# A hybrid attention and mLSTM encoder layer: v transposes two steps later, the mLSTM state split one step earlier, attention's v gathered ahead of its scores

## Chip, core and metric

The kernel runs on one core of one Trainium2 chip. The core has TensorE (PE in the profile, with its weight loads shown apart as PEld), VectorE (DVE), ScalarE (ACT), GpSimd (POOL) and SyncE (SP), whose queue issues all of this kernel's DMAs. Matmuls write into PSUM, eight banks of 128 x 512 floats; everything else lives in SBUF or in DRAM. The metric is the time of one execution on the device in microseconds. Three runs of the kernel before gave 2636.76 us in the median (2635.14 to 2638.74).

## What is computed

One layer of an encoder on two sequences, 1024 tokens (prompt) and 256 tokens (sample), model width 2048. Two groups of heads work side by side on one projection of the normalised input.

```python
hn = rmsnorm(x, norm_w)
proj = jnp.einsum('btd,dp->btp', hn, w_in)            # 2048 -> 9232 columns
na_q, na_k, na_v, na_g, ml_qk, ml_v, ml_o, ml_z, ml_gp = jnp.split(proj, cuts, axis=-1)
att = neighbourhood_attention(na_q, na_k, na_v, na_rpb)   # 8 heads of 128, windows of 8 x 16 on a grid 64 wide
att = att * jax.nn.silu(na_g)
qk = jax.nn.silu(centred_depthwise_conv(ml_qk, conv_w, conv_b))
mq, mk = jnp.split(qk, 2, axis=-1)                    # 4 heads of 256
h = bidirectional_mlstm(mq, mk, mv, gates)            # chunks, forward and backward, state C carried over chunks
mem = rmsnorm(h, head_norm_w) * sigmoid(ml_o) * silu(ml_z)
y = rmsnorm(x + concat(att, mem) @ w_out)
```

The mLSTM output of a chunk is the sum of a part inside the chunk, `p @ v`, and a part from the state carried in, `q @ C_prev`; both once forward and once backward. All of it is float32.

## The kernel before

**Precision.** To multiply float32 on TensorE, each operand is split into a high part, rounded to fp32r, and a low part, the remainder; three products (high x high, high x low, low x high) are added up. `split` (L149) makes the two parts: one copy on ACT, one subtraction on DVE. Nearly every operand goes through such a split, so a matmul waits for a DMA, then ACT, then DVE.

**Stages.** The span has three stages.

*Stage 1* (0 to about 1114 us) projects the first 768 tokens, two blocks of 128 columns at a time. `pair_a` (L314) makes one pair with seven sums of products in seven PSUM banks (three tagged `pr`, four of the five tagged `a`), in four rounds r over the contraction. In each round it goes through the seven banks; for each it splits a weight block and issues six products. In the last round `fold` adds the banks up on DVE into the result tiles `Cn` (two tiles of tag `pc`, of five) and scales them (`out_scaled`, L161). What is left to do with a pair is returned as a generator, `finish_a` (L284), and driven inside the next pair: after the banks 5, 4 and 2 of the rounds 0 to 2 `pair_a` calls `next(bg, None)` once (L380), nine steps in all, and what then remains runs behind the last round. For the eight v pairs (n1 = 56, 58, ... 70) `finish_a` has six steps: each transposes 128 tokens of the two result tiles on TensorE into the spare `a` bank (L308), copies them on ACT (L310) and stores them (L311). The pairs run in the order qk, v, rest, rest, eight times.

*Stage 2* (about 1114 to 2222 us) projects the remaining 512 tokens (`proj_v` L578, `proj_pair` L497) and does attention and mLSTM. For each of four head groups the projections come first; then `run` (L1132) takes two streams of units: the mLSTM of one head (sample, then prompt: four state units and four output units) and the attention of two heads (`na_sample`, `na_prompt`). A unit is a generator; in each turn of `run` every stream starts one more unit, and every unit already started makes one step, the newest first. So a `yield` says in which turn, and behind which other unit, an instruction is written.

*Stage 3* (about 2222 us to the end) is the output projection; the edits don't touch it.

**What sets the order.** The program is written once from top to bottom, and every instruction gets a rank in that order; what `run` writes stands under `tc.high_priority()` (L1135) and ranks ahead of all projections. A planner in the framework (`schedule_with_timeline_sim=True`, L1461) then walks through an estimated timeline and puts, on each engine, the highest-ranking instruction that it takes to be ready next. It also hands out the tiles: a tag has a fixed number of tiles, and an instruction whose tile isn't free yet is not placed until an earlier user of one is. The order so made is fixed: on the chip each engine, and SP's queue, runs its list in order and waits at its head.

**Tiles around the change.** In stage 2 mLSTM units share eight tiles of tag `hf` (L600): an output unit takes three for k, v and q, and two for the split states `Cf` (forward) and `Cr` (backward, named Cb in the profile). The state units take from the same eight. Attention's raw loads share two tiles of tag `nraw`: q and k of a head (`setup`, L686), v of a sample head, and the v gather of a block. The split v has two tiles of tag `nv`, the bias table two of tag `nbt`.

**The steps of the units.** An output unit (`out_unit`, L979) has four: load and split k, v, q (mlp_Jk, mlp_Jv, mlp_Jq); scores (mlp_Js) and the weighted in-chunk matrix (mlp_Jd, mlp_Jp); state update (L1031), state split, the products with the state (mlp_Jin) and inside the chunk (mlp_Jacc), and the normalisation (mlp_Jx, mlp_Jr, mlp_Jhs); transposes and the gate (mlp_Jtp, mlp_Jzr). An attention block (`block`, L706) has three: scores and softmax (nap_0s, nap_0st) with the gather of v; transposes of the probabilities (nap_0t, nap_0pt); the product with v (nap_0o).

Of the kernel before, what the change touches and what calls it, by code (L numbers as in the profile page):

```python
# [9 lines left out]
F32R = mybir.dt.float32r  # L10
# [3 lines left out]
P = 128  # L14
# [3 lines left out]
TP = 1024  # L18
# [20 lines left out]
def kernel(  # L39
# [17 lines left out]
    V, S, G, PE, DM = nc.vector, nc.scalar, nc.gpsimd, nc.tensor, nc.sync  # L57
# [8 lines left out]
    def bank(tag, name):  # L66
        return ps.tile([P, 512], F32, tag=tag, name=name, bufs=3 if tag == "pr" else 5)

    pT = [dram.tile([P, TT], F32, tag=f"pT{n}", name=f"pT{n}") for n in range(NCH)]
    vD = [dram.tile([TT, 256], F32, tag=f"vD{u}", name=f"vD{u}") for u in range(NU)]  # L70
# [78 lines left out]
    def split(hi, lo, src, scale=None):  # L149
        if scale is None:  # L150
            S.copy(hi, src)  # L151
            V.tensor_tensor(lo, src, f(hi), op=ALU.subtract)  # L152
        else:
            S.mul(hi, src, scale)
            V.scalar_tensor_tensor(lo, src, scale, f(hi), op0=ALU.mult, op1=ALU.subtract)
# [34 lines left out]
    def pc(name):  # L190
        return wa.tile([P, GA], F32, tag="pc", name=name, bufs=NPC)
# [75 lines left out]
    def conv_taps(dst, src, ct, n, pad):  # L267
        S.activation(
            dst[:, :n], src[:, 2 - pad : 2 - pad + n], AF.Identity,
            bias=cb_sb[:, ct : ct + 1], scale=cw_sb[:, ct, 2:3],  # L270
        )
        for j in (0, 1, 3, 4):
            a = max(pad - j, 0)
            V.scalar_tensor_tensor(  # L274
                dst[:, a:n], src[:, a + j - pad : n + j - pad], cw_sb[:, ct, j : j + 1],
                dst[:, a:n], op0=ALU.mult, op1=ALU.add,
            )
            yield
        S.activation(src[:, :n], dst[:, :n], AF.Tanh, scale=0.5)
        V.scalar_tensor_tensor(  # L280
            dst[:, :n], src[:, :n], 1.0, dst[:, :n], op0=ALU.add, op1=ALU.mult
        )

    def finish_a(n1, Cn):  # L284
        nm = f"A{n1}"
        for j in range(2):
            if n1 >= NCH:
                break
            if QK0 <= n1 < OT0:
                ct = n1 - QK0 + j  # L290
                DM.dma_start(qb[ct], Cn[j][:, GA - 4 :])
                cv = pc(f"{nm}cv{j}")
                yield from conv_taps(cv, Cn[j], ct, GA - 2, 2)
                DM.dma_start(cD[ct][:, : GA - 2], cv[:, : GA - 2])
            else:
                if OT0 <= n1 < ZT0:
                    S.activation(Cn[j], Cn[j], AF.Tanh, scale=0.5)
                elif n1 >= GT0:
                    th = pc(f"{nm}th{j}")
                    S.activation(th, Cn[j], AF.Tanh, scale=0.5)  # L300
                    V.scalar_tensor_tensor(Cn[j], th, 1.0, Cn[j], op0=ALU.add, op1=ALU.mult)
                DM.dma_start(pT[n1 + j][:, 0:GA], Cn[j])
            yield
        if n1 >= NCH:
            for tt in range(GA // P):
                b = bank("a", f"{nm}v{tt}")
                for j in range(2):
                    PE.transpose(b[:, j * P : (j + 1) * P], Cn[j][:, tt * P : (tt + 1) * P], ident)  # L308
                o = wa.tile([P, 256], F32, tag="vo", name=f"{nm}vo{tt}", bufs=2)
                S.copy(o, b[:, :256])  # L310
                DM.dma_start(vD[(n1 - NCH) // 2][tt * P : (tt + 1) * P, :], o)  # L311
                yield
# [287 lines left out]
    def hf(name):  # L600
        return ap.tile([P, 1032], F32R, tag="hf", name=name, bufs=8)
# [7 lines left out]
    def na_tile(tag, shape, name, bufs, dt=F32):  # L609
        return ap.tile(shape, dt, tag=tag, name=name, bufs=bufs)  # L610
# [71 lines left out]
    def na_prompt(h):  # L682
        nm = f"nap{h}"
        hd = {}

        def setup():  # L686
            t = na_tile("nqk", [P, 4, TP], f"{nm}qk", 1, F32R)
            q, k = ([t[:, 2 * i + z] for z in range(2)] for i in range(2))
            for half in range(2):
                cs = slice(half * 512, half * 512 + 512)  # L690
                for w_, t, src in (("q", q, pT[QT0 + h]), ("k", k, pT[KT0 + h])):
                    raw = na_tile("nraw", [P, 512], f"{nm}{w_}r{half}", 2)
                    DM.dma_start(raw, src[:, cs])
                    if w_ == "q":
                        d = [
                            x_[:, cs].rearrange("p (b r c) -> p r b c", b=4, c=16) for x_ in t
                        ]
                        split(*d, raw.rearrange("p (r b c) -> p r b c", b=4, c=16))
                    else:
                        split(t[0][:, cs], t[1][:, cs], raw)  # L700
            o = na_tile("not", [P, TP], f"{nm}o", 1)
            DM.dma_start(o[:, :GA], pT[GT0 + h][:, :GA])
            hd["q"], hd["k"], hd["o"] = q, k, o
            yield

        def block(c4):  # L706
            q, k = hd["q"], hd["k"]
            n2 = f"{nm}_{c4}"
            kc = KC0[c4]
            kv = [x_.rearrange("p (r c) -> p r c", c=64) for x_ in k]  # L710
            st = [
                na_softmax(
                    f"{n2}_{rh}",
                    lambda a_: q[a_][:, rh * 512 + c4 * P : rh * 512 + (c4 + 1) * P],
                    lambda b_: kv[b_][:, 4 * rh : 4 * rh + 12, kc : kc + 32],
                    NAK, h, (BKIND[c4] * 2 + rh) * NAK,
                )
                for rh in range(2)
            ]
            v = na_tile("nv", [P, 2, 512], f"{n2}v", 2, F32R)  # L720
            raw = na_tile("nraw", [P, 512], f"{n2}vr", 2)
            vs = vD[h // 2][:TP, (h % 2) * P : (h % 2 + 1) * P].rearrange("(r c) d -> r c d", c=64)
            for m in range(4):
                DM.dma_start(raw[:, m * P : (m + 1) * P], vs[4 * m : 4 * m + 4, kc : kc + 32, :])
            split(v[:, 0], v[:, 1], raw)
            yield
            pt = na_tile("npt", [P, 2, 768], f"{n2}pt", 1, F32R)
            for rh in range(2):
                na_transpose(
                    f"{n2}_{rh}", st[rh], ((1, 2, 0), (0, 1, 2))[rh],  # L730
                    [
                        pt[:, z].rearrange("p (s r q) -> p s r q", r=2, q=P)[:, :, rh, :]
                        for z in range(2)
                    ],
                )
            yield
            b = bank("a", f"{n2}o")
            parts = ((1, 0, 256, 0), (2, 256, 256, 0), (0, 512, P, 0), (3, 640, P, P))
            for j, (m, src, n, o) in enumerate(parts):
                for i, (a_, b_) in enumerate(((0, 0), (0, 1), (1, 0))):  # L740
                    PE.matmul(  # L741
                        b[:, o : o + n], v[:, a_, m * P : (m + 1) * P], pt[:, b_, src : src + n],
                        start=j == 0 and i == 0, stop=j == 3 and i == 2,
                    )
            ov = hd["o"].rearrange("p (r c) -> p r c", c=64)
            bv = b[:, :256].rearrange("p (r c) -> p r c", c=16)
            cs = slice(c4 * 16, c4 * 16 + 16)
            ng = GA // 64
            V.scalar_tensor_tensor(
                ov[:, :ng, cs], bv[:, :ng], 0.5, ov[:, :ng, cs], op0=ALU.mult, op1=ALU.mult  # L750
            )
            S.copy(ov[:, ng:, cs], bv[:, ng:])
            if c4 == 3:
                DM.dma_start(mixT[h][:, :TP], hd["o"])
            yield

        yield setup()
        for c4 in range(4):
            yield block(c4)
# [133 lines left out]
    def ml_units(sq, h, gates):  # L893
# [31 lines left out]
        def c_split(name, src):  # L925
            t = hf(name).rearrange("p (h t c) -> p h t c", h=2, c=VW)
            split(t[:, 0], t[:, 1], src)
            return t
# [50 lines left out]
        def out_unit(J):  # L979
            n2 = f"{nm}_{J}"  # L980
# [18 lines left out]
            for st in range(2):  # L999
# [7 lines left out]
                for d in range(2):  # L1007
# [17 lines left out]
                    split(ph[:, 0], ph[:, 1], dd)  # L1025
                    for e in range(lo_ // P, hi_ // P):
                        pp[d, e, st] = ph[:, :, e * P - lo_ : (e + 1) * P - lo_]
            yield
            if J > 0:
                if J > 1:  # L1030
                    V.scalar_tensor_tensor(  # L1031
# [3 lines left out]
                Cf = c_split(f"{n2}Cf", kvf[J - 1])  # L1035
            if J in Cb:
                Cr = c_split(f"{n2}Cb", Cb[J])
            acc = {}
            for d in range(2):
                hc = d * 4 + h  # L1040
# [26 lines left out]
            r = ap.tile([P, 8], F32, tag="smr", name=f"{n2}r", bufs=4)  # L1067
            for e in range(2):
                for d in range(2):
                    hc = d * 4 + h  # L1070
                    c = e * 2 + d
# [48 lines left out]
        for J in range(nc_):  # L1120
            yield out_unit(J)
# [344 lines left out]
```

## Time and profile before

| | us |
|---|---|
| median of three runs | 2636.76 |
| profiled execution, its own time | 2639.76 |
| span of the profiled execution | 2637.7 |
| TensorE busy, of the span | 2582.4 |
| weight loads busy | 2364.1 |
| VectorE busy | 1923.2 |
| ScalarE busy | 1309.2 |
| GpSimd busy | 709.1 |

The profile is of one execution. Its rows give an instruction group with its line in the code, what it writes and reads, how often, its busy time and mean duration, and, behind a bar, how long the engine stood idle just before it and what ended that wait. A timeline row begins with the start in us from the span's start and the duration; a bracket gives the idle time before it and its releaser. SPq is SP's queue while it issues DMAs. The end of a matmul is modelled, so TensorE's busy share says less than the starts of its instructions and the waits of the weight path.

### The profile page before, as it was taken

To read this page: it belongs to the slowest core of one execution; us is meant where nothing else is said; L and a number is where in the kernel's file an instruction comes from. 1 tells how busy PE (TensorE), PEld (TensorE's weight loads), DVE (VectorE), ACT (ScalarE), POOL (GpSimd) and SP (SyncE) were. 2 spreads that over 40 slices of the span, in tenths; PEclk is the share of its full clock that TensorE was granted. 3 is DMA by queue.
4 is the path that set the end of the run, shared out by engine and by line. 5 is a ranking of instruction groups with operands and counts; after the bars stand their busy time and mean duration, and the time that the engine had idled before them with its cause. 6 is when DMAs were issued, how large, how long until landed. Compare 5 with 4: busy or idle time off the path is not lost.

```text
span 2637.7 us, 42477 instructions
## 1 busy us (share of the span) xinstructions
PE 2582.4 (98%) x14470; PEld 2364.1 (90%) x14470; DVE 1923.2 (73%) x3744; ACT 1309.2 (50%) x2988; POOL 709.1 (27%) x951
## 2 busy tenths in 40 slices
PE   8999999999999999999999999999999999999998
PEld 8999999999999999988998998989888888787777
DVE  7858778787878778774586587677566644989796
ACT  7534444444444444543565566566566423344435
POOL 0434444444444444300011011010000000436232
PEclk9999999999999999999999999999999999999999
DMA  6423333233333232444655646655554567445327
GB/s 209 150 77 118 107 124 112 95 99 101 95 96 109 77 114 91 163 122 147 193 158 172 198 146 190 201 154 177 186 183 150 178 227 278 158 124 189 103 78 254
DMA packets 215648, 389.10 MB, mean 148 GB/s; under 512 B 26976, under 2 KB 116232, under 8 KB 215432
## 3 DMA queue, kind: packets, MB, share of 16 engines
q1 hardware_dynamic: 215432, 386.40, 46.0%
q8 instruction: 114, 1.87, 0.3%
q14 instruction: 102, 0.84, 0.1%
HBM read 314.94 MB, written 71.38 MB: 146 GB/s over the span
## 4 chain that ended last, share of the span: by engine, by line
PE 45%; DVE 8%; DMA 4%; ACT 2%; issue 1%; SPq 1%; POOL 0%; ACTq 0%; POOLq 0%; DVEq 0%
PE pc L497 21%; PE po L1300 10%; PE pv L578 4%; DVE mo L152 2%; DVE wo L152 1%; PE A54b L188 1%; DMA wr<-in_w_in_dram 1%; DVE ms L1214 1%; PE A52b L188 1%; DVE y L1250 1%; PE nap_0s L615 1%; PE nap_1s L615 1%; DMA nap_0vr<-vD 0%; DVE mb L1237 0%; PE nap_2o L741 0%
## 5 line engine op out<-in xcount | busy, mean ns | idle before, releaser
L1300 PE MATMUL po<-wo,mo 128*128 128x512 f32 x1620 | 381.0, 395 | 12.5 <-DVE wo L152 9.9
L1300 PEld LDWEIGHTS po<-wo,mo 128*128 128x128 f32 x1620 | 303.8, 188 | 88.9 <-DVE wo L152 14.9
L152 DVE TENSOR_TENSOR ws<-wr,ws 128x512 fp32r<-128x512 f32 x224 | 153.3, 695 | 119.3 <-ACT ws L151 118.0
L151 ACT CAST ws<-wr 128x512 fp32r<-128x512 f32 x224 | 136.6, 619 | 179.1 <-PE pc L497 116.8
L151 ACT CAST mo<-mb 128x640 fp32r<-128x640 f32 x72 | 51.8, 725 | 108.1 <-PE po L1300 92.4
L152 DVE TENSOR_TENSOR mo<-mb,mo 128x640 fp32r<-128x640 f32 x72 | 72.9, 1023 | 38.8 <-ACT mo L151 38.8
L1250 DVE TENSOR_TENSOR y<-y,po 128x512 f32<-128x512 f32 x90 | 57.6, 678 | 12.8 <-PE po L1300 12.8
L151 ACT CAST mo<-ms 128x640 fp32r<-128x640 f32 x40 | 29.0, 725 | 70.8 <-PE po L1300 32.5
L102 POOL TENSOR_SCALAR mls_0r<-mls_0r 128x2 f32<-128x2 f32 x4 | 1.2, 289 | 234.0 <-ACT mls_0jk L1087 234.0
L152 DVE TENSOR_TENSOR mo<-ms,mo 128x640 fp32r<-128x640 f32 x40 | 48.5, 1214 | 13.2 <-ACT mo L151 13.2
L1265 POOL TENSOR_TENSOR y<-y,fnb 128x512 f32<-128x512 f32 x30 | 48.1, 1621 | 36.3 <-ACT jk L1263 35.8
L152 DVE TENSOR_TENSOR wsv<-wr_v,wsv 128x512 fp32r<-128x512 f32 x64 | 44.0, 693 | 17.5 <-ACT wsv L151 16.8
L151 ACT CAST wsv<-wr_v 128x512 fp32r<-128x512 f32 x64 | 38.9, 617 | 30.8 <-PE pc L497 19.2
L165 DVE TENSOR_TENSOR pco<-pc,rstdb 128x512 f32<-128x512 f32 x48 | 32.8, 686 | 27.8 <-PE pc L497 26.1
L1227 POOL TENSOR_TENSOR wb_0a<-wb_0a,wb_0b 128x512 f32<-128x512 f32 x2 | 2.6, 1302 | 179.5 <-DMA wb_0b<-in_w_o_dram 179.5
L274 DVE SCALAR_TENSOR_TENSOR pcv<-pco,cw_sb,pcv 128x516 f32<-128x516 f32 x64 | 46.7, 749 | 0.0
L1214 DVE TENSOR_TENSOR ms<-mb,mb 128x640 f32<-128x640 f32 x40 | 45.1, 1127 | 0.0
L1263 ACT ACTIVATE jk<-y 128x512 f32<-128x512 f32 x40 | 25.2, 631 | 39.7 <-DVE y L1250 38.2
L497 PE MATMUL pc<-x_0h,ws 128*128 128x512 f32 x112 | 36.5, 406 | 0.9 <-DVE pco L165 0.9
L497 PE MATMUL pc<-x_2h,ws 128*128 128x512 f32 x112 | 35.3, 399 | 0.0
L188 PE MATMUL fb<-xb,fw 128*128 128x384 f32 x96 | 24.7, 374 | 10.8 <-ACT xb L158 10.8
L188 PE MATMUL fb<-xg,fw 128*128 128x384 f32 x192 | 35.1, 336 | 0.1
(1701 smaller groups left out, 8268.9 us busy)
## 6 DMA issues: line engine op xcount, KB each, us to landing
wr<-in_w_in_dram SPq DMA_DIRECT2D x112, 512.0 KB
wr_v<-in_w_in_dram SPq DMA_DIRECT2D x32, 512.0 KB
xq<-in_xtok_dram SPq DMA_DIRECT2D x20, 512.0 KB
mb<-mx SPq DMA_DIRECT2D x32, 320.0 KB
y<-in_xtok_dram SPq DMA_DIRECT2D x40, 256.0 KB
wr_wp<-in_w_o_dram SPq DMA_DIRECT2D x16, 512.0 KB
xr<-in_xT_dram SPq DMA_DIRECT2D x16, 384.0 KB
nap_0bt<-in_rpb_tab_dram SPq DMA_DIRECT2D x32, 192.0 KB
```

What stands on the lines that cost most here:

```text
L151: S.copy(hi, src)
L152: V.tensor_tensor(lo, src, f(hi), op=ALU.subtract)
L165: V.tensor_tensor(o, src, rb, op=ALU.mult)
L188: PE.matmul(o, w(a_), x(b_), start=first and m == 0, stop=last and m == 2)
L274: V.scalar_tensor_tensor(dst[:, a:n], src[:, a + j - pad : n + j - pad], cw_sb[:, ct, j : j + 1], dst[:, a:n], op0=ALU.mult, op1=ALU.add,)
L497: PE.matmul(pb[j], t[j][:, wi, c : c + P], xs[xi], start=first and m == 0, stop=last and m == 2,)
L578: PE.matmul(outs[tt], xs[:, tt * P : (tt + 1) * P], t[:, wi, q * w : (q + 1) * w], start=first and m == 0 and (gates or tt % 2 == 0), stop ...
L615: PE.matmul(b[:, :nkeys], qs(a_), ks(b_), start=i == 0, stop=i == 2)
L1214: V.tensor_tensor(t, x, y_, op=op)
L1250: V.tensor_tensor(Y[p, q, tt], Y[p, q, tt], bk, op=op)
L1265: G.tensor_tensor(Y[p, q, tt], Y[p, q, tt], fnb[c], op=ALU.mult)
L1300: PE.matmul(bk[tt], m[xi][:, tt * P : (tt + 1) * P], w[wi], start=first and kk == 0 and j == 0, stop=last and j == 2, skip_group_check=True,)
```

## The change

There are three edits. The number of instructions is the same; only their place in the program's order changes.

```diff
@@ finish_a
         if n1 >= NCH:
+            yield
+            yield
             for tt in range(GA // P):
                 b = bank("a", f"{nm}v{tt}")
@@ block (attention of a prompt head)
             kv = [x_.rearrange("p (r c) -> p r c", c=64) for x_ in k]
+            v = na_tile("nv", [P, 2, 512], f"{n2}v", 2, F32R)
+            raw = na_tile("nraw", [P, 512], f"{n2}vr", 2)
+            vs = vD[h // 2][:TP, (h % 2) * P : (h % 2 + 1) * P].rearrange("(r c) d -> r c d", c=64)
+            for m in range(4):
+                DM.dma_start(raw[:, m * P : (m + 1) * P], vs[4 * m : 4 * m + 4, kc : kc + 32, :])
             st = [
                 na_softmax(
...
                 for rh in range(2)
             ]
-            v = na_tile("nv", [P, 2, 512], f"{n2}v", 2, F32R)
-            raw = na_tile("nraw", [P, 512], f"{n2}vr", 2)
-            vs = vD[h // 2][:TP, (h % 2) * P : (h % 2 + 1) * P].rearrange("(r c) d -> r c d", c=64)
-            for m in range(4):
-                DM.dma_start(raw[:, m * P : (m + 1) * P], vs[4 * m : 4 * m + 4, kc : kc + 32, :])
+            yield
             split(v[:, 0], v[:, 1], raw)
-            yield
             pt = na_tile("npt", [P, 2, 768], f"{n2}pt", 1, F32R)
@@ out_unit (mLSTM)
                         pp[d, e, st] = ph[:, :, e * P - lo_ : (e + 1) * P - lo_]
-            yield
             if J > 0:
                 if J > 1:
                     V.scalar_tensor_tensor(
...
                 Cf = c_split(f"{n2}Cf", kvf[J - 1])
             if J in Cb:
                 Cr = c_split(f"{n2}Cb", Cb[J])
+            yield
             acc = {}
```

Edit 1: the generator of a v pair makes two empty steps first, so that its transposes, copies and stores come two steps later in the next pair. Edit 2: the state update and the splits of both states come at the end of an output unit's second step instead of the start of its third. Edit 3: the four gather DMAs of an attention block come before its scores and the loads of its bias tables, and the split of the gathered v comes behind the step, ahead of the transposes of the probabilities.

## The prediction

> **What bounds the kernel now.** I read the page's busy shares first, then the same shares by stage, since the three edits lie in two of three stages.
>
> ```profile
> span 2637.7 us, 42477 instructions
> PE 2582.4 (98%) x14470; PEld 2364.1 (90%) x14470; DVE 1923.2 (73%) x3744; ACT 1309.2 (50%) x2988; POOL 709.1 (27%) x951
> ...
> core 0: us, PE busy (x) PEld busy (x) DVE busy (x) ACT busy (x) POOL busy (x), PEclk, DMA share, GB/s
> 0.00:1114.00 1114.00, 1094.94 (x6273) 1084.50 (x6274) 869.62 (x1566) 529.47 (x1241) 469.33 (x560) 1.00 0.36 113
> 1114.00:2222.00 1108.00, 1093.26 (x6519) 964.52 (x6518) 718.25 (x1785) 604.17 (x1427) 80.11 (x277) 1.00 0.56 177
> 2222.00:2637.70 415.70, 394.22 (x1682) 315.07 (x1680) 335.32 (x396) 175.52 (x320) 159.70 (x114) 0.99 0.49 162
> ```
>
> TensorE is the bound in all three stages at full granted clock; DVE has about a fifth of each stage free, ACT and the DMA engines over 40%. So an instruction moved on ACT, DVE or the DMA queue has no price of its own: only time in which TensorE then stands still counts. The third stage (out-projection) isn't touched. The question is which TensorE stalls in the first two stages go, and which come.
>
> **Edit 1: v transposes two steps later (stage 1).** The cost of today's place is seen by comparing pairs. A64 is a v pair; its transposes run inside the next pair, A40. First starts:
>
> ```profile
> L188 PE MATMUL A40b<-xb,A40s x24: 331/336/423, 695.1 to 720.5; 128*128 128x384 f32 x24
> ...
> L188 PE MATMUL A42b<-xb,A42s x24: 331/335/342, 727.0 to 749.7; 128*128 128x384 f32 x24
> ...
> L188 PE MATMUL A34b<-xb,A34s x24: 331/335/342, 756.1 to 778.8; 128*128 128x384 f32 x24
> ```
>
> The pair behind a v pair lasts 727.0 - 695.1 = 31.9 us, the following one 756.1 - 727.0 = 29.1. Of the 2.8 us between them, part is the transposes themselves, the rest a wait:
>
> ```profile
> 699.45 0.91 DVE L165 TENSOR_TENSOR A64c<-A64c,rstdb 128x384 f32<-128x384 f32 x1
> ...
> 700.41 0.14 PEld L308 LDWEIGHTS A64v<-ident,A64c 128*128 128x128 f32 x1 [0.92 <-DVE A64c L165]
> 700.41 0.33 PE L308 MATMUL A64v<-ident,A64c 128*128 128x128 f32 x1 [0.60 <-DVE A64c L165]
> ...
> 701.42 0.55 DVE L165 TENSOR_TENSOR A64c<-A64c,rstdb 128x384 f32<-128x384 f32 x1
> ...
> 707.06 0.32 PEld L308 LDWEIGHTS A64v<-ident,A64c 128*128 128x128 f32 x2
> ...
> 707.35 4.01 PEld L188 LDWEIGHTS A40b<-xg,A40s 128*128 128x128 f32 x23
> ```
>
> Two transposes that wait for nothing take 707.35 - 707.06 = 0.29 us of the weight path, so twelve take 1.74 us and stay wherever they are put; 2.8 - 1.74 = 1.06 us are left. That agrees with the wait in the row: the first transpose came when DVE had not yet scaled the v pair's result, and the weight path stood 0.92 us. The same wait stands in front of each of the eight v pairs:
>
> ```profile
> L308 PEld LDWEIGHTS A58v<-ident,A58c 128*128 128x128 f32 x12 | 1.7, 140 | 1.1 <-DVE A58c L165 0.9
> L308 PE MATMUL A58v<-ident,A58c 128*128 128x128 f32 x12 | 2.5, 276 | 0.6 <-DVE A58c L165 0.6
> ```
>
> A step is two banks of six products; at 4.01/23 = 0.174 us each that is 2.1 us, so the first transpose moves to about 700.4 + 4.2 = 704.6. The last scaling of A64c ends at 701.42 + 0.55 = 701.97, before that. All four halves are scaled by then, so the later groups wait for nothing either. Nine steps are there before the pair's last round and eight will be used, so none is pushed into the next pair; the two PC tiles are held some 4 us longer, with one of five still free. PE then meets the next pair's own weight splits, which the pairs without transposes meet with no stall. Gain: 8 x 0.92 = 7.4 us; bounds 8 x 0.60 = 4.8 (matmul row) and 8 x 1.06 = 8.5 (pair difference). I take 7.4, the wait on the path that feeds every product.
>
> The Trainium skill ("TensorE: Matmul & The Clock Gate", section "Back-to-back issue gap") gives some 81 ns for a 128-wide product in a stream of weight load and matmul. By it twelve transposes would be an estimated 0.97 us, the wait 1.8 us a pair and the gain 14.6; the trace has 145 ns each and a wait of 0.92 in its own record, so the trace decides.
>
> **Edit 2: mLSTM state split one step earlier (stage 2).** Moved are, in each of four head groups, three forward and three backward splits (one ACT and one DVE instruction each) and two state updates on DVE; no DMA. Today's stalls on the weight path, whole stage:
>
> ```profile
> PEld mlp_1in L919 <- ACT mlp_1Cf L151: 3.3, 3, 1.6
> PEld nap_0s L615 <- ACT mlp_1x L1052: 2.2, 2, 1.9
> ...
> PEld mlp_2in L919 <- DVE mlp_0zr L1108: 1.4, 2, 0.9
> ...
> PEld mlp_1in L919 <- ACT mlp_1Cb L151: 1.2, 1, 1.2
> ...
> PEld nap_0s L615 <- ACT nap4qk L151: 1.0, 1, 1.0
> ...
> PEld mlp_2in L919 <- DVE mlp_3d L1022: 0.7, 1, 0.7
> ```
>
> Why is Cf late? Its source was ready long before: the next unit's state update, which reads the same tile, ran 49 us ahead of the split. The program's order is only a rank, and the planner pulls ready work forward:
>
> ```profile
> L1031 DVE SCALAR_TENSOR_TENSOR mlp0a1kf<-mlp0a0kf,mgpso,mlp0a1kf x1: 741/741/741, 1333.7 to 1333.7; 128x516 f32<-128x516 f32 x1
> ...
> L152 DVE TENSOR_TENSOR mlp_1Cf<-mlp0a0kf,mlp_1Cf x1: 690/690/690, 1383.0 to 1383.0; 128x516 fp32r<-128x516 f32 x1
> ...
> 1381.70 0.63 ACT L154 ACTIVATE mlp_3q<-mlp_3qcv 128x512 fp32r<-128x512 f32 x1 [1.51 <-DMA mlp_3qcv<-cD]
> 1382.24 0.61 ACT L151 CAST mlp_1Cf<-mlp0a0kf 128x516 fp32r<-128x516 f32 x1
> ...
> POOL mlp_3v L911 <- PE mlp_0in L919: 11.8, 4, 3.9
> ```
>
> What the split lacks is one of the eight "hf" tiles, which units hand on (the last row: unit 3's v waits for unit 0's products), and it stands on ACT behind unit 3's q, which waits 1.51 us for a DMA. With the edit Cf and Cb of unit 1 rank ahead of unit 3's k, v, q, so their rows (3.3 + 1.2 = 4.5 us) should go. In exchange unit 3's v and q get a tile only from unit 1's products, and unit 2's splits rank behind them: the two mlp_2in rows (2.1) may grow. Bounds: all four rows gone, -6.6; all moved splits stalling, +22.8 (worked out as a rival). I take -2: the 4.5 of the rows less 2.5 for what is late next, unit 2.
>
> **Edit 3: v gather ahead of the scores, its split behind the step (stage 2).** In each of 32 blocks four gather DMAs now rank ahead of the two bias-table loads, and one ACT and one DVE split (0.62 and 0.69 us) go behind the step. On the DMA queue today:
>
> ```profile
> 1375.65 0.54 SPq L724 DMA_DIRECT2D nap_0vr<-vD  x1
> 1376.53 0.85 SPq L903 DMA_DIRECT2D mlp_3qcv<-cD  x2
> 1377.43 2.58 SPq L724 DMA_DIRECT2D nap_0vr<-vD  x3
> 1380.11 1.06 SPq L724 DMA_DIRECT2D nap_1vr<-vD  x2
> ...
> 1385.05 2.74 SPq L724 DMA_DIRECT2D nap_2vr<-vD  x4
> 1387.83 1.13 SPq L474 DMA_DIRECT2D wr<-in_w_in_dram  x2
> ...
> 1393.43 0.62 ACT L151 CAST ws<-wr 128x512 fp32r<-128x512 f32 x1 [5.66 <-DMA wr<-in_w_in_dram]
> ...
> L151 ACT CAST nap_0v<-nap_0vr 128x512 fp32r<-128x512 f32 x8 | 5.0, 620 | 17.4 <-DMA nap_0vr<-vD 13.9 <-DMA nap_1vr<-vD 2.9 <-issue 0.6
> L151 ACT CAST nap_2v<-nap_2vr 128x512 fp32r<-128x512 f32 x8 | 4.9, 614 | 8.7 <-PE nap_0o L741 8.7
> ```
>
> Gathers are already issued far ahead of their scores (three blocks of one head within 13 us), because only the two raw tiles hold them. So the edit's lead on the queue is small: past two bias loads. What changes is the raw tile, which is now kept across a step. Good: the third block's gather (2.74 us of issue) can no longer go ahead of the weight load whose lateness (ACT waits 5.66) cost PE the 1.9 us of nap_0s, and the ACT waits of the last two rows shrink, which lie under other work of PE. Bad: the next head's q and k loads use the same two raw tiles, and behind them on SP stand weight loads. Bounds: -3.2 (both nap_0s rows gone) to +8 (each of eight heads waits for its q/k as nap_0s does once today, 1.0). I take 0.
>
> **Sum.** The profiled execution has 2639.8 us around its span of 2637.7. 2639.8 - 7.4 - 2 - 0 = 2630.4. It lies 3.0 above the median 2636.8 of the runs, so in terms of the median 2627.4.
>
> **Rivals.** *Given back:* the raw tiles delay each head's q/k as above, +8, and edit 2 wins its 2: 2636.8 - 7.4 - 2 + 8 = 2635.4. For it: two raw tiles serve four users. Against: the projections' products are there to fill any wait the planner foresees; only waits that it misjudges cost.
>
> *Slower:* the moved splits take the hf tiles early and come to the head of ACT before a tile is free; ACT issues in order, so weight splits and PSUM evictions stand behind. Today one such ACT wait of 5.66 us cost PE 1.9. With one at each of the 12 forward splits: +22.8, so 2636.8 - 7.4 + 22.8 = 2652.2. It decides from four such stalls on (4 x 1.9 = 7.6 eats edit 1); from about seven on, the kernel is slower by what can be measured (7 x 1.9 - 7.4 = 5.9). For it: eight tiles against the ten that units need by then (v, q, Cf, Cb; k, v, q; k, v, q). Against: three of four groups stall today for the opposite reason. The Trainium skill (the clock-gate page, section "Architectural detail") calls ACT's queue a strict FIFO, which is what the mlp_3q and mlp_1Cf rows show.
>
> *It doesn't do what it says:* a yield only changes rank; the planner may put the transposes where DVE is late again, and edit 2 and half of edit 1 remain: 2636.8 - 2 - 3.7 = 2631.1, or 2636.8 with nothing. Against: in stage 1 PE has ready products all the time, so rank is place.
>
> *All stalls named go:* -8.5 - 6.6 - 3.2 = -18.3: 2618.5.
>
> **How the numbers follow.** Forecast 0.52, given back 0.20, slower 0.16, doesn't do 0.05, all stalls go 0.07. What a measurement can tell from no change is about 0.2%, 5.3 us: below 2631.5 is faster, above 2642.1 slower. Nearly all of the forecast, the last rival and a fifth of "given back" are faster: 0.59; the rest of "given back", "doesn't do" and the forecast's upper edge are same: 0.24; slower 0.17. The forecast's own range is 2622 to 2632; the range that should hold is 2618 (all stalls go) to 2642 (it includes "given back" and the first part of "slower").
>
> **What would show it.** Stage 1: pairs behind a v pair lasting 30.9 instead of 31.9 us, and no DVE releaser in front of L308; stage 1 ends 7 us earlier. Stage 2: no mlp_1in waiting for Cf or Cb, their ACT splits ahead of mlp_3q; new stalls at mlp_3s, mlp_2in or nap_0s would be edits 2 and 3 given back. I am wrong if stage 1 isn't shorter, or stage 2 moves by more than 8 us either way.

## The result and the profile after

The changed kernel takes 2611.69 us in the median of five runs (2610.53 to 2614.36), against 2636.76 of before (2633.03 to 2638.86, five runs beside it): a ratio of 0.9911, with a 95% interval of 0.9900 to 0.9922. It is faster, as forecast, but by 25 us where 9.4 were forecast, and lies below the range.

The page's first two lines of the changed kernel, and then its busy shares in four stretches: up to the first product of pair A6, to the first pv product (end of stage 1), to the first po product (end of stage 2), to the end.

```profile
span 2611.8 us, 42439 instructions
PE 2571.7 (98%) x14470; PEld 2361.3 (90%) x14470; DVE 1930.9 (74%) x3744; ACT 1311.1 (50%) x2988; POOL 706.1 (27%) x951
...
0.00:116.00 116.00, 101.32 (x557) 98.08 (x558) 90.61 (x161) 78.00 (x153) 24.69 (x33) 1.00 0.60 191
116.00:1102.70 986.70, 986.70 (x5717) 983.70 (x5716) 788.70 (x1405) 451.83 (x1089) 442.93 (x527) 1.00 0.33 105
1102.70:2196.00 1093.30, 1088.97 (x6521) 963.21 (x6520) 717.90 (x1785) 606.16 (x1427) 79.27 (x277) 1.00 0.57 179
2196.00:2611.80 415.80, 394.74 (x1681) 316.32 (x1679) 333.65 (x396) 175.12 (x320) 159.18 (x114) 0.98 0.49 161
```

The same stretches of the kernel before, cut at the same events:

```profile
0.00:117.30 117.30, 104.14 (x557) 100.84 (x558) 91.05 (x161) 77.67 (x153) 24.48 (x33) 0.97 0.61 189
117.30:1113.90 996.60, 990.70 (x5717) 983.56 (x5716) 778.47 (x1406) 451.80 (x1088) 444.85 (x527) 1.00 0.33 104
1113.90:2222.20 1108.30, 1093.56 (x6521) 964.78 (x6519) 718.55 (x1785) 604.17 (x1427) 80.11 (x277) 1.00 0.56 177
2222.20:2637.70 415.50, 394.02 (x1681) 314.91 (x1679) 335.12 (x396) 175.52 (x320) 159.70 (x114) 0.99 0.49 162
```

The first number behind the bounds is the length. The five engines execute the same number of instructions in both (the page's total of 42439 against 42477 also counts instructions that are not work), so all that differs is time without work: 996.6 to 986.7 in stage 1 (-9.9), 1108.3 to 1093.3 in stage 2 (-15.0), stage 3 as before. The first stretch is 1.3 shorter at a clock of 1.00 instead of 0.97; no edit reaches it, and in the other profiles it ends anywhere from 115.0 to 116.6.

**Stage 1.** First starts of the three pairs shown in the prediction, then the start of the v transposes in the changed kernel's timeline, and their group (L310 is L308 of before).

```profile
L188 PE MATMUL A40b<-xb,A40s x24: 331/335/423, 689.1 to 713.0; 128*128 128x384 f32 x24
...
L188 PE MATMUL A42b<-xb,A42s x24: 331/335/342, 719.7 to 742.4; 128*128 128x384 f32 x24
...
L188 PE MATMUL A34b<-xb,A34s x24: 331/335/342, 748.8 to 771.5; 128*128 128x384 f32 x24
```

```profile
693.42 0.91 DVE L165 TENSOR_TENSOR A64c<-A64c,rstdb 128x384 f32<-128x384 f32 x1
...
695.14 0.14 PEld L310 LDWEIGHTS A64v<-ident,A64c 128*128 128x128 f32 x1
...
L310 PEld LDWEIGHTS A64v<-ident,A64c 128*128 128x128 f32 x12 | 1.7, 140 | 0.2
```

The pair behind a v pair now lasts 719.7 - 689.1 = 30.6 us (31.9 before), the other 29.1 as before. The first transpose starts 6.0 us into the pair (5.3 before), 0.8 us after the scaling it reads; no DVE releaser is left. In the order of the weight path it stood behind 24 weight loads of its pair before and stands behind 36 now, in each of the eight v pairs: 12 products later, which is one step. A second wait of the weight path is gone too. It stood some 3 us ahead of the first transpose, in front of a product of the same pair; the first row is from before, the second from the changed kernel, where the loads run through:

```profile
697.45 1.00 PEld L188 LDWEIGHTS A40b<-xg,A40s 128*128 128x128 f32 x6 [0.42 <-issue]
...
689.94 5.21 PEld L188 LDWEIGHTS A40b<-xg,A40s 128*128 128x128 f32 x30
```

Both waits, 0.92 and 0.42 us, recur in each of the eight pairs that follow a v pair. The list of the weight path's waits for stage 1 sums to 10.9 us before and 1.1 after, so 9.8 of the 9.9 us are waits.

**Stage 2.** The weight path's waits in stage 2 of the changed kernel: who waited for whom, us in total, times, longest.

```profile
PEld mlp_3tp L1096 <- DVE nap_1sm L622: 2.7, 2, 1.9
PEld nap_0s L617 <- ACT mlp3a2kf L968: 1.4, 1, 1.4
PEld mlp1a2kv L921 <- POOL mlp1a0v L915: 1.0, 1, 1.0
PEld mgpmc L826 <- issue: 0.7, 2, 0.4
PEld mgsmc L826 <- issue: 0.7, 2, 0.4
PEld mlp2a2kv L921 <- issue: 0.7, 1, 0.7
PEld mlp_1acc L921 <- ACT mlp_1x L1054: 0.4, 1, 0.4
```

With the smaller rows it is 8.7 us; the same list of before has 22.1. All six rows of before that the prediction shows are gone. Of those that it left out, these have shrunk or gone, from 7.8 us in all to 2.5 (nap_0s 1.4, mlp2a2kv 0.7, the two pc rows 0.2 each; mlp1a2kv has 1.0 with another releaser, which is not counted here); one, mlp_3tp, has grown from 0.9 to 2.7:

```profile
PEld nap_0s L615 <- ACT mlp3a2kf L966: 2.2, 1, 2.2
...
PEld mlp2a2kv L919 <- issue: 1.9, 1, 1.9
...
PEld mlp1a2kv L919 <- issue: 1.4, 1, 1.4
PEld pc L497 <- DVE pco L165: 1.2, 1, 1.2
...
PEld pc L497 <- ACT ws L151: 1.1, 1, 1.1
```

The state split of unit 1 and unit 3's q split in the changed kernel (first start is that of the first head group):

```profile
L151 ACT CAST mlp_1Cf<-mlp0a0kf x1: 622/622/622, 1347.8 to 1347.8; 128x516 fp32r<-128x516 f32 x1
...
L154 ACT ACTIVATE mlp_3q<-mlp_3qcv x4: 632/633/635, 1365.5 to 1981.1; 128x512 fp32r<-128x512 f32 x4
```

Cf now comes 17.7 us ahead of mlp_3q, where before it stood right behind it (1382.24 and 1381.70). It comes so early that ACT now waits for its tile, which unit 0's products give back: 4.6 us in all, in three of the four head groups.

```profile
ACT mlp_1Cf L151 <- PE mlp_0in L921: 4.6, 3, 1.8
```

### The profile page after: what moved, and what is told of

It is laid out like the page before. It is cut to its first block, busy times and chain, and to the rows that moved or that the text cites. A ratio compares the mean times of both kernels' runs of the same rounds, so it can differ in the third digit from the quotient of the medians.

```text
span 2611.8 us, 42439 instructions
## 1 busy us (share of the span) xinstructions
PE 2571.7 (98%) x14470; PEld 2361.3 (90%) x14470; DVE 1930.9 (74%) x3744; ACT 1311.1 (50%) x2988; POOL 706.1 (27%) x951
## 4 chain that ended last, share of the span: by engine, by line
PE 82%; DVE 7%; DMA 6%; ACT 2%; issue 1%; POOL 1%; SPq 1%; ACTq 0%; POOLq 0%; DVEq 0%
PE pc L499 20%; PE po L1302 10%; PE pv L580 5%; DVE mo L152 1%; DVE wo L152 1%; PE A24b L188 1%; PE A16b L188 1%; PE A8b L188 1%; PE A12b L188 1%; PE A20b L188 1%; PE A52b L188 1%; PE A48b L188 1%; PE A44b L188 1%; PE A40b L188 1%; PE A70b L188 1%
## 5 line engine op out<-in xcount | busy, mean ns | idle before, releaser
L1302 PE MATMUL po<-wo,mo 128*128 128x512 f32 x1620 | 381.8, 396 | 12.1 <-DVE wo L152 10.2
L1302 PEld LDWEIGHTS po<-wo,mo 128*128 128x128 f32 x1620 | 305.3, 189 | 87.8 <-DVE wo L152 14.3
L152 DVE TENSOR_TENSOR mo<-ms,mo 128x640 fp32r<-128x640 f32 x40 | 47.3, 1183 | 13.4 <-ACT mo L151 13.4
L188 PEld LDWEIGHTS fb<-xg,fw 128*128 128x128 f32 x192 | 33.3, 188 | 2.2 <-ACT xg L158 2.2
```

The costliest lines, as they stand in the source:

```text
L188: PE.matmul(o, w(a_), x(b_), start=first and m == 0, stop=last and m == 2)
L1302: PE.matmul(bk[tt], m[xi][:, tt * P : (tt + 1) * P], w[wi], start=first and kk == 0 and j == 0, stop=last and j == 2, skip_group_check=True,)
```

## The experiments

All ratios are to runs of the kernel before on the same chip, with 95% intervals; "stage 2" is the time from the first pv to the first po product in the profile (before: 1108.3).

**Edit 1 alone.**

```diff
         if n1 >= NCH:
+            yield
+            yield
             for tt in range(GA // P):
```

> Edit 1 alone (v transposes two steps later). The changed kernel's first stage ended 11.2 us earlier than before's (first pv product at 1102.7 instead of 1113.9) and its second stage was 15.0 us shorter. Theory 'own place' (each edit moves only its own stage): 2625 to 2627 us, -10 to -11, pairs behind a v pair at 30.8 us, second stage 1108 us as before. Rival 'reshuffle' (any edit gives the planner a new order for the second stage, and before's was an unlucky one): second stage shorter here too, by 5 us or more, total under 2620.

Ratio 0.9963 (0.9951 to 0.9976), 2624.4 us. Stage 1 is 986.6 us long from A6 on, as in the changed kernel; stage 2 is 1105.2, its list of waits 20.9 us with mostly the rows of before. Of the 3.1 us, 1.2 are waits and most of the rest a dip of the clock that before has in its stage 2 and this run doesn't (shown below). So edit 1 acts in its own stage.

**Edit 2 alone.**

```diff
-            yield
             if J > 0:
...
                 Cr = c_split(f"{n2}Cb", Cb[J])
+            yield
```

> Edit 2 alone (state update and splits one step earlier). First stage as before. Theory 'state split carries it': second stage 10 to 15 us shorter, 2622 to 2627, no mlp_1in wait, and the stalls at nap_0s and kv shrink with it because ACT isn't behind. Rival 'each its own rows': only the mlp_1in rows go (4.5 us), 2632. Rival 'tiles run out': mlp_3s or mlp_2in wait more than the 2.1 us of before and nothing is won, 2637.

Ratio 0.9967 (0.9954 to 0.9979), 2626.0 us; stage 2 is 1096.8, at the lower end of the first theory. The largest waits of the weight path in stage 2:

```profile
PEld mlp_1acc L919 <- ACT mlp_1x L1052: 4.2, 4, 1.8
PEld pc L497 <- DVE ws L152: 1.7, 2, 1.4
PEld nap_0s L615 <- ACT mlp3a2kf L966: 1.4, 1, 1.4
```

No mlp_1in and no mlp_2in wait is left; the largest new row is mlp_1acc (4.2). The sum is 12.2 us instead of 22.1. The rivals fall: more went than the split's own rows, and the tiles did not run out.

**Edit 3 alone.** (The hunk of `block` in the change.)

> Edit 3 alone (v gather ahead of the scores, split behind the step). First stage as before. Theory 'state split carries it': within 3 us of before, 2634 to 2638, mlp_1in waits still there. Rival 'gather carries it': second stage 10 to 15 us shorter, 2622 to 2627, because weight loads no longer stand behind three blocks of gathers. My prediction had 0 for it, with +8 as the bad end.

Ratio 0.9979 (0.9969 to 0.9989), 2628.6 us; stage 2 is 1099.8, waits 12.9 us. Neither theory as put: edit 2 is not the only one that counts, and the mlp_1in waits are still there (3.0 us). Which half of the edit it is, is answered below.

**Edits 2 and 3 together.**

> Edits 2 and 3 without edit 1. If stages are independent: 2636.8 - 15 = 2622, second stage 1093 us, first stage ending at 1114. If edit 1 has a share in the second stage: less than 15, 2625 or more. Against the two single runs: additive if s2 and s3 together make 15; if each alone gives nearly as much as both, they remove the same waits.

Ratio 0.9951 (0.9936 to 0.9965), 2622.3 us. Stage 2 is 1096.5, waits 10.2 us: in the profile hardly shorter than with edit 2 alone. By the profiles, the two edits remove partly the same waits: in stage 2 they win 11.5 and 8.5 alone, and together 11.8. This run also has a clock dip there that the run of edit 2 has not. In time, edit 1's 0.37% and the pair's 0.49% make 0.86%, close to the 0.89% of the change: the stages add up. For the edits inside stage 2 the times don't decide: edit 2's 0.33% and edit 3's 0.21% make 0.54%, which lies inside the pair's interval (0.35% to 0.64%). That the two remove the same waits is what one profile of each says, not what the times show.

**The two halves of edit 3.** First the gathers' rank alone, the split still ahead of the step:

```diff
             kv = [x_.rearrange("p (r c) -> p r c", c=64) for x_ in k]
+            v = na_tile("nv", [P, 2, 512], f"{n2}v", 2, F32R)
+            raw = na_tile("nraw", [P, 512], f"{n2}vr", 2)
...
+                DM.dma_start(raw[:, m * P : (m + 1) * P], vs[4 * m : 4 * m + 4, kc : kc + 32, :])
             st = [
```

> Half of edit 3: the four gathers ahead of the scores, the v split still ahead of the step. Edit 3 alone made the second stage 8.5 us shorter (1099.8 against 1108.3). Theory 'rank of the gather' (the loads come earlier on SP and ACT no longer waits for them): most of it is here, 2628 to 2631. Rival 'place of the split' (ACT and DVE no longer wait at their head for the gather or for a free v tile): nothing here, 2633 to 2637.

Ratio 0.9998 (0.9989 to 1.0007): nothing. The gathers hardly start earlier for it: in the first four heads, the first issue of each block stays within 1.5 us of its place in stage 2 of before. Then the split's place alone (s3_split in the texts below):

```diff
+            yield
             split(v[:, 0], v[:, 1], raw)
-            yield
```

> The other half of edit 3: gathers behind the scores as before, the v split behind the step. Theory 'place of the split': ACT waits in front of nap_0v (17.4 us) and nap_2v (8.7) fall below 5 us together, second stage 6 to 9 us shorter, 2626 to 2630. Rival 'rank of the gather': 2633 to 2637.

Ratio 0.9968 (0.9955 to 0.9980), 2626.6 us, stage 2 1099.6: all of edit 3. ACT's idle time in front of the v splits stands behind the last bar, first in the kernel with the gathers moved, then in that with the split moved:

```profile
L151 ACT CAST nap_0v<-nap_0vr 128x512 fp32r<-128x512 f32 x8 | 5.0, 620 | 16.7 <-DMA nap_0vr<-vD 16.0 <-issue 0.6
...
L151 ACT CAST nap_2v<-nap_2vr 128x512 fp32r<-128x512 f32 x8 | 4.9, 615 | 8.5 <-PE nap_0o L741 8.5
L151 ACT CAST nap_3v<-nap_3vr 128x512 fp32r<-128x512 f32 x8 | 4.9, 613 | 1.9 <-PE nap_1o L741 1.9
```

```profile
L151 ACT CAST nap_2v<-nap_2vr 128x512 fp32r<-128x512 f32 x8 | 5.0, 630 | 0.0
...
L151 ACT CAST nap_3v<-nap_3vr 128x512 fp32r<-128x512 f32 x8 | 5.0, 626 | 0.0
...
L151 ACT CAST nap_0v<-nap_0vr 128x512 fp32r<-128x512 f32 x8 | 4.9, 618 | 18.4 <-DMA nap_0vr<-vD 13.3 <-DMA nap_1vr<-vD 5.0
```

The wait for a gather (nap_0v) stays, and the gain comes all the same; the wait for one of the two nv tiles, which the product of an earlier block gives back (nap_2v, nap_3v), is gone. My expectation that the waits at nap_0v and nap_2v would fall below 5 us together was half wrong.

The wait for a tile is not costly by itself, though. With edit 2 alone ACT still waits 8.6 us at nap_2v and 1.6 at nap_3v, and TensorE's waits are no longer than with the split moved (12.2 us against 14.3).

**Two orders without a price.** The first is p_swap, the second p_load.

```diff
-                    DM.dma_start(o_, pT[OT0 + ch][:, c0 : c0 + na])
                     DM.dma_start(zn, pT[ZT0 + ch][:, c0 : c0 + na])
+                    DM.dma_start(o_, pT[OT0 + ch][:, c0 : c0 + na])
```

> A change with no price of its own: in an output unit's last step the loads of the two gate tiles are swapped; the instruction that uses them needs both. Theory 'mechanism' (edits 2 and 3 win by their own rows): within 3 us of before, 2631 to 2637. Rival 'reshuffle' (the second stage's stalls are where the planner's estimate misses, any new order redraws them, and before's was a poor draw): 5 us or more faster, with other rows in the list of waits than before's.

```diff
-            cv = load_c(n1, 8 + 2 * h, J)
             vt = load_v(n1, J, hf(f"{n1}v"))
+            cv = load_c(n1, 8 + 2 * h, J)
```

> A second change with no price of its own: in a state unit v is loaded ahead of k instead of behind it; both are needed before the unit's products. Theory 'mechanism': 2631 to 2637. Rival 'reshuffle': 5 us or more away from before, either way; if p_swap and p_load land on both sides of before, the spread between them is what a redrawn order is worth, and the second stage's gain by edits 2 and 3 has to be larger than that to be called theirs.

Ratios 1.0006 (0.9997 to 1.0015) and 0.9990 (0.9981 to 0.9998); stage 2 1106.5 and 1104.4. The redrawn orders moved the time by 0.06% and 0.10% (by the intervals at most 0.2%), a third or less of the 0.33% and 0.32% of edit 2 and the split's place. In a single profile a redrawn order can shorten stage 2 by up to 3.9 us, so smaller differences between two profiles show nothing. The rival that before's order was a poor draw falls, as far as two draws can tell.

**Which blocks.** The split's place moved for blocks 2 and 3 of each head alone, then for 0 and 1 alone:

```diff
-            split(v[:, 0], v[:, 1], raw)
+            if c4 < 2:
+                split(v[:, 0], v[:, 1], raw)
             yield
+            if c4 >= 2:
+                split(v[:, 0], v[:, 1], raw)
```

> Of edit 3 only the split of blocks 2 and 3 of each head is put behind the step; gathers and the splits of blocks 0 and 1 stay. Before has ACT waits of 8.7 us at nap_2v and 2.3 at nap_3v (for one of the two nv tiles), 17.4 at nap_0v (for its DMA). Theory 'waiting for a tile': the whole gain of s3_split is here, second stage 1099 to 1101, 2626 to 2628. Rival 'waiting for the DMA': nothing here, 2633 to 2637. If the splits only have to rank lower anywhere, about half: 2630 to 2632.

> The complement: only blocks 0 and 1 put behind the step. Theory 'waiting for a tile': as before, 2633 to 2637, with nap_2v still waiting 8.7 us. Rival 'waiting for the DMA': 2626 to 2629 and less wait at nap_0v.

Ratios 0.9972 (0.9963 to 0.9981) and 0.9985 (0.9976 to 0.9995); stage 2 1101.9 and 1101.5. The first agrees with "waiting for a tile": no wait is left at blocks 1 to 3, nap_0v still waits 19.0 us, and the whole gain is there. The second should have won nothing and won about half. Its ACT waits:

```profile
L151 ACT CAST nap_2v<-nap_2vr 128x512 fp32r<-128x512 f32 x8 | 5.1, 640 | 0.0
L151 ACT CAST nap_0v<-nap_0vr 128x512 fp32r<-128x512 f32 x8 | 5.0, 621 | 12.5 <-DMA nap_0vr<-vD 11.3 <-issue 1.1
L151 ACT CAST nap_1v<-nap_1vr 128x512 fp32r<-128x512 f32 x8 | 5.0, 619 | 5.4 <-PE nap_0o L744 5.3
L151 ACT CAST nap_3v<-nap_3vr 128x512 fp32r<-128x512 f32 x8 | 4.9, 610 | 2.3 <-PE nap_1o L744 2.3
```

With blocks 0 and 1 later, nap_2v too no longer waits, but nap_1v now does, for the same product nap_0o (5.4 us, 0.0 before); nap_3v waits as before. So the waits for a tile went from 11.0 us to 7.7, not to nothing, and half a gain fits that. But nap_0v's wait is less here as well (12.5 instead of 17.4), so the two causes are not cleanly parted in this run. Its single profile also doesn't rank the two kernels as the times do: stage 2 has 13.3 us of waits and two dips here, 17.1 and none in the first.

**Which output units.**

```diff
-            yield
+            if J > 1:
+                yield
             if J > 0:
...
                 Cr = c_split(f"{n2}Cb", Cb[J])
+            if J < 2:
+                yield
```

> Edit 2 for output units 0 and 1 only; units 2 and 3 split their states a step later as before. Edit 2 alone made the second stage 11.5 us shorter (1096.8). Theory 'unit 1 is the late one' (only the mlp_1in rows show the wait, unit 2 and 3 find their tiles anyway): 1097 to 1099, 2625 to 2628, no mlp_1in wait. Rival 'units 2 and 3 count too': half of it, 2629 to 2632, with mlp_2in waits of 2 us or more left.

Ratio 0.9971 (0.9961 to 0.9981), 2626.5 us, stage 2 1099.2 with waits of 12.5 us and one clock dip: as good as the whole edit 2, and no mlp_1in and no mlp_2in wait is left. Units 2 and 3 needn't split earlier. That unit 1 is the late one is read from the rows of before, where no wait at mlp_0in stands; units 0 and 1 were not tried apart, nor were Cf and Cb.

**The v split later still, on top of all three edits.**

```diff
-            split(v[:, 0], v[:, 1], raw)
             pt = na_tile("npt", [P, 2, 768], f"{n2}pt", 1, F32R)
...
+            split(v[:, 0], v[:, 1], raw)
             yield
             b = bank("a", f"{n2}o")
```

> All three edits, and the v split still later: behind the transposes of the probabilities instead of ahead of them. In the changed kernel nap_0v still waits 11.6 us on ACT for its gather. If that wait stands in front of work PE needs: 2 to 4 us faster than the changed kernel (2611.7), 2608. If the 11.6 us lie beside other work, as 17 us did in s3_split: 2611 to 2613. If the product with v now waits for its split: 2616 or more, with a wait at nap_0o.

Ratio 0.9898 (0.9884 to 0.9911), 2607.6 us: the lowest median here. Stage 2 is 1091.2 with 6.4 us of waits (changed kernel 1093.3 and 8.7). Not as the first sentence of the expectation has it, though: nap_0v's wait is 13.1 us, no less than the 11.6 of the changed kernel. The row that shrank most is mlp_3tp waiting for DVE's nap_1sm, from 2.7 to 0.9 us. Against the changed kernel's ratio, taken at another time, the intervals overlap, so that it beats it by 0.1% is likely, not shown.

**Does it add up?** Stage 2 of every profile, less the sum of its weight-path waits, less 1.7 us for each dip of the clock (how the 1.7 comes about stands in the last section):

| kernel | stage 2 | waits | dips | left |
|---|---|---|---|---|
| before | 1108.3 | 22.1 | 1 | 1084.5 |
| edit 1 | 1105.2 | 20.9 | 0 | 1084.3 |
| edit 2 | 1096.8 | 12.2 | 0 | 1084.6 |
| edit 3 | 1099.8 | 12.9 | 1 | 1085.2 |
| gathers only | 1106.7 | 20.0 | 1 | 1085.0 |
| split only | 1099.6 | 14.3 | 0 | 1085.3 |
| p_swap | 1106.5 | 18.9 | 2 | 1084.2 |
| p_load | 1104.4 | 18.8 | 1 | 1083.9 |
| split of blocks 2 and 3 | 1101.9 | 17.1 | 0 | 1084.8 |
| split of blocks 0 and 1 | 1101.5 | 13.3 | 2 | 1084.8 |
| edit 2 for units 0 and 1 | 1099.2 | 12.5 | 1 | 1085.0 |
| edits 2 and 3 | 1096.5 | 10.2 | 1 | 1084.6 |
| all three (after) | 1093.3 | 8.7 | 0 | 1084.6 |
| v split later still | 1091.2 | 6.4 | 0 | 1084.8 |

Within 1.4 us the rest is the same in each. So the 15.0 us by which stage 2 is shorter in the two profiles are 13.4 us of TensorE waits and one dip, and nothing else of that size.

## Why the prediction was right or wrong

*The bound* was right: TensorE's time is the kernel's time in stages 1 and 2, and moved instructions had no price of their own. One reading was off without consequence: in stage 2 DVE is busy for 718 of 1108 us, so a third is free there, not a fifth.

*Edit 1* had the right mechanism and a term too small: 7.4 us, bounds 4.8 to 8.5, against 9.9. The mis-sized term is the wait of 0.92 us a pair. The pair behind a v pair became 1.3 us shorter, and the weight path has two waits there, 0.92 and 0.42 us; I read only the record in front of the transposes and missed the other, which stands in a row of the pair's own products. The pair difference hid it, because the price of a transpose was too high: I took 0.29 us for two from one spot, 1.74 for twelve, and left 1.06 us a pair, which seemed to agree with 0.92. Without these waits the pair is 30.6, that is 1.5 us over 29.1, so a transpose costs 1.5/12 = 0.12 us. The record of the 0.42 us names no releaser; why that wait goes with the edit stays open. The place was wrong too: the first transpose moved by 12 products of the weight path's order, some 2.1 us of work, and not by two steps of 4.2. That was enough to come behind the scaling.

*Edit 2*: the step that failed is "the 4.5 of the rows less 2.5 for what is late next, unit 2". Unit 2 was not late next: its two rows (2.1) went as well. And the stated best end of 6.6 counted only the four rows at mlp_1in and mlp_2in. Alone, the edit took 9.9 us out of the waits (22.1 to 12.2): rows at nap_0s, kv (the products for the state) and pc (the projection) went or shrank as well. That they went because they stood behind the same ACT and DVE queues is the likely reason; no run shows it by itself. The mechanism (Cf on ACT ahead of unit 3's q) is shown by the starts, and by units 0 and 1 carrying the edit. The *slower* rival's condition, splits at the head of ACT without a tile, did come about: ACT waits 4.6 us there in the changed kernel. But it had no price that shows: mlp_3s and mlp_2in have no wait of note.

*Edit 3*: the step that failed is that the ACT waits of the two quoted rows "lie under other work of PE", so "I take 0". It held for the larger one, nap_0v, which is as long when the gain is there. It did not hold for the smaller one, nap_2v: with the split moved and that wait gone, stage 2 is 8.7 us shorter in the profile, and the time 0.32%. The bad end of +8, q and k of the next head behind the two raw tiles, did not show, and the good reason that I gave, fewer gathers ahead of a weight load, was not the one: the gathers' rank alone is worth nothing that can be measured.

*Sum and range*: the errors all lay on one side, since each edit was priced by a few rows of the list, with something given back, and a list of 22 us was taken for 10. The two terms of stage 2, -2 and 0, measured -15.0 in the profile, beyond the 8 us that the prediction gave as its own sign of being wrong. The *all stalls named go* rival (2618.5) came nearest, and the measured time is below it too, for the same reason.

What stays open: by which of ACT's and DVE's queued instructions a wait of nap_2v becomes a wait of kv or nap_0s some microseconds later. The runs show that the waits of TensorE go when the split is moved, not each link. Since edit 2 removes as much while nap_2v still waits, that wait seems to cost only where ACT is already late for something that TensorE needs; that is argued, not shown.

## What to carry to other kernels

Where an engine issues in order and feeds the bound engine, a wait for a tile at its head can't be priced by its own rows: here 8.7 us of it (nap_2v) went together with 8.7 us of stage 2, while 17 to 19 us of waiting for a gather stayed in kernels that had the gain. Price such an edit by the bound engine's whole list of waits in that stage, and let its best end be the whole list. A stage's length less the bound engine's waits should come out the same for all variants; where it does, the accounting is closed, and what is left in the list is all that order can still win. Writing a DMA issue earlier was worth nothing here, because the transfers hardly started earlier for it; what paid was to write its consumer, which holds up its engine, where its buffer is already free.

## What the runs showed of the hardware

Short stalls of TensorE can cost more than their length. The kernel before in three windows of 12 us, with the granted clock as the third number from the end, and PE's timeline in the second:

```profile
2000.00:2012.00 12.00, 12.00 (x64) 10.25 (x63) 6.62 (x16) 5.47 (x12) 1.98 (x4) 1.00 0.40 119
2012.00:2024.00 12.00, 10.27 (x49) 8.26 (x48) 8.27 (x18) 6.63 (x13) 0.00 (x0) 0.86 0.57 189
2024.00:2036.00 12.00, 12.00 (x66) 10.23 (x64) 7.80 (x26) 5.39 (x16) 0.90 (x2) 1.00 0.53 168
```

```profile
2015.75 0.50 PE L497 MATMUL pc<-x_0l,ws 128*128 128x512 f32 x1 [0.84 <-ACT ws L151]
2016.08 0.90 PE L497 MATMUL pc<-x_0h,ws 128*128 128x512 f32 x2
2017.87 1.17 PE L497 MATMUL pc<-x_0h,ws 128*128 128x512 f32 x2 [0.89 <-DVE pco L165]
```

Two waits of PE of under 1 us each (1.1 and 1.2 on the weight path), and the clock over the window is 0.86: 0.14 x 12 = 1.7 us lost on top. Cut into single microseconds, the clock is 0.50 from 2018 to 2021 and 0.82 in the one after. Every dip in stage 2 of the other profiles costs the same 1.7 us and begins within 3 us of the end of a wait of PE, some of them a single one (1.86 us in the run of edits 2 and 3). Other waits, the longest 2.2 us on the weight path and 1.8 on PE (nap_0s in the kernel before), brought no dip, and the variants have it at other places or not at all. The Trainium skill ("TensorE: Matmul & The Clock Gate", section "Why this matters for your kernels") advises against idle gaps of over some 3 us; here gaps well below that were followed by a dip, so a stall is to be priced with a chance of 1.7 us on top.
